# Part-array steps of the first group in larger sets: decode value sums, retention reads, state updates

## The chip, the core and the metric

The kernel runs on one core of a Trainium2 chip, in one launch. The metric is the device time in microseconds; three runs were made. A profile of one more execution shows every instruction with its start and length.

The core has five engines that work at the same time, each through its own instructions in order: TensorE (PE; its weight loads are shown as PEld), VectorE (DVE), ScalarE (ACT), GpSimd (POOL) and SyncE (SP, which only issues transfers here). Matmul results land in PSUM, which this kernel uses as eight banks of 128 x 512 fp32 values.

## The reference

One step of a layer with two groups of eight heads, 128 wide each, in fp32. A prompt of 1024 frames and eight running streams of 16 new frames ("sample") pass through it. Group A is stick-breaking attention, group B is retention with a state per head:

```python
def stick_breaking_block(q, k, v, q_start):
    z = einsum('bqhd,bkhd->bhqk', q, k) * HEAD_DIM ** -0.5
    strict = (k_pos[None, :] < q_pos[:, None])
    log_beta = log_sigmoid(z)
    log_keep = where(strict, log_sigmoid(-z), 0.0)
    later = cumsum(log_keep, axis=3, reverse=True) - log_keep
    a = where(strict, exp(log_beta + later), 0.0)
    return einsum('bhqk,bkhd->bqhd', a, v)

def retention_chunk(q, k, v, s, log_gamma):
    scores = einsum('bihd,bjhd->bhij', q, k) * intra
    o = einsum('bhij,bjhe->bihe', scores, v)
    o = o + einsum('bihd,bhde->bihe', q, s) * decay_read
    s_new = s * exp(lg * n) + einsum('bjhd,hj,bjhe->bhde', k, decay_write, v)
    return o, s_new

def reference(...):
    # prompt and sample alike:
    h = rms_norm(x, norm_pre)
    q_sb, k_sb, v_sb, gate_sb, q_r, k_r, v_r, gate_r = split(h @ w_in)   # 2048 x 8192; rope on q_r, k_r
    o_sb = stick_breaking(...)     # sample: over 1024 cached keys and values and its own 16
    o_r, s = retention(...)        # sample: from state_ret
    y = concat(head_rms_norm(o_sb) * silu(gate_sb), head_rms_norm(o_r) * silu(gate_r))
    x = x + rms_norm(y @ w_out, norm_post)
    # also returned: new keys, values and states
```

## The kernel before

Frames are taken in tiles of 128: eight of the prompt (0 to 7) and one that holds all eight sample streams (16 frames each). The first group is tiles 0 to 3 and the sample tile, the second is tiles 4 to 7. For each group the kernel goes through the eight heads. A head has its projections ("products", `products` and `project_rows`, lines 229 and 288): each is a long chain of matmuls over 16 input tiles, in three terms of a high and low split, into banks called `acc` or `accn`. A weight tile is loaded by SP (`wr`), split by ScalarE (`wh`) and VectorE (`wl`), four tiles ahead. After both groups comes the output projection.

Everything else of a head is cut into small steps and put between the products. A step sequence is a Python generator in a `Job`; it yields the number of ticks until its next step. `tick()` is called behind each term of products (every two products in the first group, every three in `project_rows`), and runs at most one due job. The constants `D_...` are these counts; those with two entries are for the two groups. A scheduler then sets the final order of each engine's instructions, which the order listings show.

The steps that the change touches are all in the first group, since only that one has the sample tile:

- `decode`: stick-breaking attention of the sample tile over the cache. Keys come in pieces (`kc`, by POOL), VectorE turns them (`kcT`), and twice per head a set of eight matmuls makes 512 columns of scores `zc`, for 32 rows of queries each, so four of them fill the array's columns. ScalarE evacuates them as `kp` and `be`. The weights are turned through DRAM; then the values: `pd` takes one matmul with the sample's own values (line 720) and eight key tiles of cached values `vc` (line 728), four matmuls of 32 rows each. These were written two key tiles at a time, `2 * D_VC` ticks apart. VectorE then puts together `do`.
- `sample_retention`: loads four tiles of states `st`, computes scores times values (line 812) and reads of the states (line 815, again 32 rows of the output each) into the accumulator bank `pa`, puts `ro` together on ScalarE and VectorE, and updates the states from keys of 32 frames (line 832): two sets of two tiles, in the two banks of the score pool `z`, each added to `st` by VectorE (line 835) and stored.
- `stick_breaking`: rows of prompt attention, lagged by two: scores `z` (line 588), weights turned through DRAM, and the sums with values into `pa` (line 618). `D_TR` is the pause before the last row's sums.

An fp32 matmul of these steps is two instructions in the profile. In the profile's shapes, 128*32 is a matmul on 128 rows and 32 columns of the array, 32*128 one on 32 rows and 128 columns.

## Time and profile before

| | |
|---|---|
| median of 3 runs | 2400.34 us (2395.4 to 2400.91) |
| the profiled execution | 2397.79 us, its span 2396.1 us |
| TensorE busy | 2332.6 us, 97% of the span |
| VectorE, ScalarE, GpSimd busy | 1254.6, 919.6, 646.2 us |
| mean granted TensorE clock | 0.993 of full speed |
| transfers | 418.68 MB, mean 175 GB/s |

The first group's heads run from about 165 to 1230 us. Start times in the timeline tell more than busy times here, because matmuls overlap one another in flight: the time that a step costs TensorE is read from the start of the product before it to the start of the product behind it.

### The profile page before, as it was taken

How to read it: one execution, taken by the hardware profiler on the slowest of the kernel's cores; microseconds unless marked ns; L12 is line 12 of the kernel's file. 1: busy time of each engine (PE TensorE's matmuls, PEld its weight loads, DVE VectorE, ACT ScalarE, POOL GpSimd, SP SyncE). 2: the span in 40 equal slices, each digit the busy share in tenths (PEclk: the TensorE clock that was granted, in tenths of full speed). 3: DMA queues.
4: the chain of work that ended last, by engine and by line, in shares of the span. 5: the costliest groups of instructions: out<-in, count | busy, mean ns of one | idle time of the engine just before them, and what ended most of it. 6: DMA issues, size and time to landing. Idle time of an engine off the chain costs nothing.

```text
span 2396.1 us, 40529 instructions
## 1 busy us (share of the span) xinstructions
PE 2332.6 (97%) x14832; PEld 2094.6 (87%) x14832; DVE 1254.6 (52%) x2442; ACT 919.6 (38%) x1937; POOL 646.2 (27%) x1033
## 2 busy tenths in 40 slices
PE   7999999999999999998899999999999999999998
PEld 7998899999999999987778888889898888888887
DVE  7245455445554555455545554555554566564544
ACT  6323333324333333324333343343343444444443
POOL 3144353444344353443302111120220220010000
PEclk9999999999999999999999999999999999999999
DMA  7658879797889879798875555556654667765553
GB/s 244 166 130 210 167 166 197 174 199 164 188 178 191 181 174 187 182 192 199 188 189 150 150 141 150 146 142 153 153 152 127 166 163 195 231 214 181 189 191 131
DMA packets 677050, 418.68 MB, mean 175 GB/s; under 512 B 224753, under 2 KB 620017, under 8 KB 674545
## 3 DMA queue, kind: packets, MB, share of 16 engines
q1 hardware_dynamic: 524272, 285.99, 47.6%
q0 software_dynamic: 32256, 71.36, 13.7%
q10 hardware_dynamic: 120320, 58.74, 9.0%
q8 instruction: 116, 1.90, 0.3%
q14 instruction: 86, 0.70, 0.1%
HBM read 336.24 MB, written 79.69 MB: 174 GB/s over the span
## 4 chain that ended last, share of the span: by engine, by line
PE 83%; DMA 7%; DVE 4%; issue 2%; ACT 2%; SPq 1%; POOL 0%; DVEq 0%; ACTq 0%; POOLq 0%
PE acc L229 44%; PE accn L288 17%; DMA mr<-s_y 4%; PE a L1031 3%; PE a L1032 3%; PE a L1030 3%; PE pa L618 3%; PE z L588 2%; DMA wr<-w_in 2%; PE zc L661 1%; PE pd L728 1%; DMA mr<-s_h 1%; DVE wl L132 1%; DVE ml L132 1%; ACT mh L131 1%
## 5 line engine op out<-in xcount | busy, mean ns | idle before, releaser
L229 PE MATMUL acc<-mh,wh 128*128 128x256 f32 (+2 forms) x2304 | 665.4, 342 | 7.8 <-ACT wh L131 5.0
L132 DVE TENSOR_TENSOR wl<-wr,wh 128x512 fp32r<-128x512 f32 (+1 forms) x576 | 391.8, 685 | 523.8 <-ACT wh L131 513.8
L229 PE MATMUL acc<-ml,wh 128*128 128x384 f32 (+2 forms) x2304 | 663.8, 341 | 0.0
L229 PE MATMUL acc<-mh,wl 128*128 128x256 f32 (+2 forms) x2304 | 660.2, 339 | 0.6 <-DVE wl L132 0.5
L131 ACT ACTIVATE wh<-wr 128x512 fp32r<-128x512 f32 (+1 forms) x576 | 357.4, 625 | 730.9 <-PE acc L229 247.7
L229 PEld LDWEIGHTS acc<-mh,wh 128*128 128x128 f32 x2304 | 420.7, 189 | 45.0 <-ACT wh L131 7.1
L229 PEld LDWEIGHTS acc<-mh,wl 128*128 128x128 f32 x2304 | 424.7, 189 | 31.6 <-issue 2.1
L229 PEld LDWEIGHTS acc<-ml,wh 128*128 128x128 f32 x2304 | 422.9, 189 | 33.2 <-issue 5.3
L645 POOL DMA_DIRECT2D kc<-cache_sb_k x512 | 331.6, 653 | 370.0 <-DVE kcT L683 205.9
L288 PE MATMUL accn<-whn,mh 128*128 128x256 f32 x1152 | 329.2, 287 | 0.6 <-ACT whn L131 0.5
L288 PE MATMUL accn<-wln,mh 128*128 128x256 f32 x1152 | 325.9, 283 | 1.5 <-DVE wln L132 1.5
L288 PE MATMUL accn<-whn,ml 128*128 128x256 f32 x1152 | 325.9, 283 | 0.0
L288 PEld LDWEIGHTS accn<-whn,mh 128*128 128x128 f32 x1152 | 220.5, 192 | 10.5 <-issue 7.5
L288 PEld LDWEIGHTS accn<-wln,mh 128*128 128x128 f32 x1152 | 220.9, 192 | 2.5 <-DVE wln L132 1.7
L288 PEld LDWEIGHTS accn<-whn,ml 128*128 128x128 f32 x1152 | 220.9, 192 | 0.0
L1031 PE MATMUL a<-wl,mh 128*128 128x512 f32 (+1 forms) x576 | 219.5, 381 | 0.2 <-DVE wl L132 0.2
L1032 PE MATMUL a<-wh,ml 128*128 128x512 f32 (+1 forms) x576 | 219.0, 381 | 0.0
L1030 PE MATMUL a<-wh,mh 128*128 128x512 f32 (+1 forms) x576 | 218.9, 381 | 0.0
L132 DVE TENSOR_TENSOR wln<-wrn,whn 128x512 fp32r<-128x512 f32 x128 | 87.5, 687 | 119.7 <-ACT whn L131 119.5
L131 ACT ACTIVATE whn<-wrn 128x512 fp32r<-128x512 f32 x128 | 80.1, 633 | 151.6 <-PE accn L288 65.4
L481 POOL DMA_DIRECT2D be<-s_be x128 | 94.0, 741 | 134.2 <-DMA s_be<-be 114.6
L1031 PEld LDWEIGHTS a<-wl,mh 128*128 128x128 f32 x576 | 108.4, 188 | 21.2 <-DVE wl L132 0.9
(189 smaller groups left out, 2611.6 us busy)
## 6 DMA issues: line engine op xcount, KB each, us to landing
wr<-w_in SPq DMA_DIRECT2D x384, 256.0 KB, 4.2
wr<-w_out SPq DMA_DIRECT2D x184, 256.0 KB, 3.6
wrn<-w_in SPq DMA_DIRECT2D x128, 256.0 KB, 3.2
kc<-cache_sb_k POOLq DMA_DIRECT2D x512, 64.0 KB, 4.6
vc<-cache_sb_v SPq DMA_DIRECT2D x64, 512.0 KB, 8.5
xt<-x_prompt SPq DMA_DIRECT2D x8, 1024.0 KB, 6.2
xr<-x_prompt SPq DMA_DIRECT2D x8, 1024.0 KB, 6.5
out<-out ACTq DMA_DIRECT2D x24, 256.0 KB, 3.6
```

Source lines behind the costliest of these rows:

```text
L131: nc.scalar.activation(hi, src, AF.Copy)
L132: nc.vector.tensor_tensor(lo, src, hi.bitcast(F32), ALU.subtract)
L229: last = nc.tensor.matmul(a[:, :m], lhs[:, j, :], rhs[w][:, j, o : o + m], start=(w == 0 and j == 0 and n == 0), stop=(w == KT // WQ - 1 a ...
L288: anchor[0] = nc.tensor.matmul(a, lhs[q][:, jj, ts], rhs[:, j, :], start=(w == 0 and j == 0 and n == 0 and t % 2 == 0), stop=(w == KT // 2 ...
L481: q.dma_start(raw[32 * i : 32 * i + 32, :].rearrange("p (k a) -> p k a", a=32), s[:, :, 32 * i : 32 * i + 32].rearrange("k (j b) a -> b (k ...
L588: nc.tensor.matmul(z[:, :c], q2[a][:, i * P : (i + 1) * P], k2[b][:, s : s + c], start=(m == 0), stop=(m == 2),)
L618: nc.tensor.matmul(po[:, :P], at[:, j, :], vn[:, j, :], start=(j == 0), stop=(j == t))
L645: nc.gpsimd.dma_start(kc[32 * i : 32 * i + 32, :].rearrange("p (k d) -> p k d", d=32), cache_k[0, 2 * c + j, s * 512 : (s + 1) * 512, h, 3 ...
L661: mm = nc.tensor.matmul(z[r, :], qp[:, j, r], ready[2 * j + c // 2][:, c % 2, :], start=(j == 0), stop=(j == 1),)
L1030: nc.tensor.matmul(a[:, :width], hi[q][:, j, ts], wh, start=(k == 0), stop=False)
L1031: nc.tensor.matmul(a[:, :width], hi[q][:, j, ts], wl, start=False, stop=False)
L1032: nc.tensor.matmul(a[:, :width], lo[q][:, j, ts], wh, start=False, stop=(k == KT - 1))
```

## The change

The value sums of a head go in two sets of four key tiles, 46 ticks apart, where there were four sets of two. The retention reads no longer stand at a place of their own: they are put in a list, and issued right behind the first set of decode scores that comes (`with_scores`), with the scores-times-values matmul behind them; head 0 keeps them where they were. If no set comes within 80 ticks they are issued anyway. The state updates go in one set with four tiles, two in the banks of the score pool, one in the accumulator bank `pa` and one in the decode bank `pd`; the order of the first two alternates by head, and the first matmuls are tied to stand in that order. The four stores follow after a pause. The pause before the last attention row in the first group is 12 ticks instead of 3, the one before the value sums 7 instead of 3, and the decode sums on VectorE wait six ticks more.

```diff
-D_TR = (3, 7)
+D_TR = (12, 7)
-D_VC = 9
+D_VC = (6, 46)
+V_SET = 4
+D_SUM = 6
+D_TD = 7
+D_OFF = 3
+N_READ = 40
...
+        waiting = []
+        def with_scores():
+            while waiting:
+                waiting.pop(0)()
...
                     ready = []
+                    with tc.issue_after(mm.ins):
+                        with_scores()
                     sigmoids(kp, be, s * 512, z)
...
-            yield D_TR[phase[0]]
+            yield D_TD
...
-            for k0 in range(0, 8, 2):
-                yield 2 * D_VC
-                for k in (k0, k0 + 1):
+            for k0 in range(0, 8, V_SET):
+                yield D_VC[k0 > 0]
+                for k in range(k0, k0 + V_SET):
                     vc = values.pop(0)
...
+            yield D_SUM
             od = out.o[:, 0, :]
...
-            po = acc_tile()
-            nc.tensor.matmul(po[:, 2 * P : 3 * P], sc, rv[:, i, :], start=True, stop=True)
-            for c in range(4):
...
-            yield D_RET[phase[0]]
+            def read_states():
+                po = acc_tile()
+                for c in range(4):
+                    r = slice(32 * c, 32 * c + 32)
+                    nc.tensor.matmul(
+                        po[r, : 2 * P], rq[:, i * P + 32 * c : i * P + 32 * c + 32], sts[c], start=True, stop=True
+                    )
+                nc.tensor.matmul(po[:, 2 * P : 3 * P], sc, rv[:, i, :], start=True, stop=True)
+                read.append(po)
+            if h:
+                waiting.append(read_states)
+                for _ in range(N_READ):
+                    if read:
+                        break
+                    yield 2
+            if not read:
+                waiting.clear()
+                read_states()
+            po = read[0]
+            yield D_OFF
...
-            for c0 in (0, 2):
-                pS = [score_tile(f"pSs{c}", (P, 2, P)) for c in range(2)]
...
+            yield D_OFF
+            pS = [score_tile(f"pSs{c}", (P, 2, P)) for c in range(2)]
+            pS += [
+                pool.tile([P, 512], F32, name=f"p{n}", tag=f"p{n}")[:, : 2 * P].rearrange("p (j e) -> p j e", j=2)
+                for pool, n in ((psa, "a"), (psd, "d"))
+            ]
+            lead = None
+            for j in range(2):
+                for c in (0, 1, 2, 3) if h % 2 else (1, 0, 2, 3):
+                    r = slice(32 * c, 32 * c + 32)
+                    with tc.issue_after(lead.ins) if lead else nullcontext():
+                        mm = nc.tensor.matmul(pS[c][:, j, :], rkn[r, i + j, :], rv[r, i, :], start=True, stop=True)
+                    if j == 0 and c < 2:
+                        lead = mm
+            for c in range(4):
+                nc.vector.scalar_tensor_tensor(
+                    sts[c], sts[c], math.exp(LOG_GAMMA[h] * DS), pS[c], ALU.mult, ALU.add
+                )
+            yield D_RET[phase[0]]
+            for c in range(4):
+                nc.scalar.dma_start(s_sample[0, 2 * c : 2 * c + 2, h].rearrange("b d e -> d b e"), sts[c])
```

The new order is read at three places, all in the head with index 4 of the first group (one of the middle heads); products are left out.

TensorE, from the value sums of that head to the first retention steps of the next, before the change (`pd` are the value sums, `rs` retention scores, `pa` the accumulator bank):

```order
L720 MATMUL pd<-vn,kp 128x128
L728 MATMUL pd<-vc,kp 32x256 x8
...
L728 MATMUL pd<-vc,kp 32x256 x8
...
L728 MATMUL pd<-vc,kp 32x256 x8
...
L754 MATMUL rs<-rq,rk 128x128
...
L754 MATMUL rs<-rq,rk 128x128
...
L728 MATMUL pd<-vc,kp 32x256 x8
...
L772 MATMUL pa<-rv,sc 128x128
```

The same stretch of TensorE after the change:

```order
L733 MATMUL pd<-vn,kp 128x128
L741 MATMUL pd<-vc,kp 32x256 x16
...
L741 MATMUL pd<-vc,kp 32x256 x16
...
L768 MATMUL rs<-rq,rk 128x128
...
L768 MATMUL rs<-rq,rk 128x128
```

Four sets of eight matmuls, with 34 to 36 products between them, have become two of sixteen with 76 products between them, and none stands behind the retention scores any more.

TensorE at the reads and updates, before (`pSs` are the update tiles, `zc` the decode scores):

```order
L812 MATMUL pa<-rv,sc 128x128
L815 MATMUL pa<-st,rq 32x256 x4
...
L832 MATMUL pSs_8266<-rv,rkn 128x128
L832 MATMUL pSs_8267<-rv,rkn 128x128
...
L832 MATMUL pSs_8315<-rv,rkn 128x128
...
L661 MATMUL zc<-kcT,qp 32x512 x8
```

and after (`z` are the scores of a prompt row):

```order
L672 MATMUL zc<-kcT,qp 32x512 x8
L831 MATMUL pa<-st,rq 32x256 x4
L834 MATMUL pa<-rv,sc 128x128
...
L866 MATMUL pSs_8375<-rv,rkn 128x128
L866 MATMUL pSs_8374<-rv,rkn 128x128
L866 MATMUL pa<-rv,rkn 128x128
L866 MATMUL pd<-rv,rkn 128x128
...
L593 MATMUL z<-kh,qh 128x256
```

The reads follow the scores with nothing between; 21 products stand between them and the one update set, and three products between that set and the next `z`, which takes the bank of the first update tile. Here the updates stood before the decode scores, now they stand behind them.

VectorE at the same place, before (`ro` is the retention output, `ov` and `or` its norm, `st` the states):

```order
L822 SCALAR_TENSOR_TENSOR ro<-pa,dec,ro 128x128 x2
L683 STREAM_TRANSPOSE kcT<-kc 128x512
L132 TENSOR_TENSOR wln<-wrn,whn 128x512
L139 TENSOR_SCALAR ov<-ssq_7506 128x5
L835 SCALAR_TENSOR_TENSOR st<-st,pSs_8266 128x256
L835 SCALAR_TENSOR_TENSOR st<-st,pSs_8267 128x256
L141 RECIPROCAL or<-or 128x5
```

and after:

```order
L851 SCALAR_TENSOR_TENSOR ro<-pa,dec,ro 128x128 x2
L696 STREAM_TRANSPOSE kcT<-kc 128x512
L144 TENSOR_SCALAR ov<-ssq_7498 128x5
L146 RECIPROCAL or<-or 128x5
L870 SCALAR_TENSOR_TENSOR st<-st,pSs_8375 128x256
L870 SCALAR_TENSOR_TENSOR st<-st,pSs_8374 128x256
L902 STREAM_TRANSPOSE kn<-kT 128x640
L870 SCALAR_TENSOR_TENSOR st<-st,pa 128x256
L870 SCALAR_TENSOR_TENSOR st<-st,pd 128x256
```

The reciprocal, which waits for ScalarE's square root, now stands ahead of the first update, and a transposition of keys stands between the second and the third.

More of the change, by code (lines that the diff above doesn't have):

```diff
@@ L730, in decode @@
                         )
-                for k in (k0, k0 + 1):
+                for k in range(k0, k0 + V_SET):
                     if k + V_BUFS < 8:
                         values.append(load_v(k + V_BUFS))
+            yield D_SUM
             od = out.o[:, 0, :]
@@ L825, in sample_retention @@
             out.done(i)
-            for c0 in (0, 2):
-                pS = [score_tile(f"pSs{c}", (P, 2, P)) for c in range(2)]
-                for j in range(2):
-                    for c in range(2):
-                        r = slice(32 * (c0 + c), 32 * (c0 + c) + 32)
-                        nc.tensor.matmul(pS[c][:, j, :], rkn[r, i + j, :], rv[r, i, :], start=True, stop=True)
-                for c in range(2):
-                    st, b = sts[c0 + c], 2 * (c0 + c)
-                    nc.vector.scalar_tensor_tensor(
-                        st, st, math.exp(LOG_GAMMA[h] * DS), pS[c], ALU.mult, ALU.add
-                    )
-                    nc.scalar.dma_start(s_sample[0, b : b + 2, h].rearrange("b d e -> d b e"), st)
-                yield D_RET[phase[0]]
+            yield D_OFF
[19 more added lines that the diff above has]
+                nc.scalar.dma_start(s_sample[0, 2 * c : 2 * c + 2, h].rearrange("b d e -> d b e"), sts[c])
         def ret_branch(gi, g, h, rq, rk, rv, rest):
```

5 lines of the change are left out of this document (1 added, 4 removed).

## The prediction

> **What bounds the kernel now.** I read the page first, then the list of waits and the table by stretch for the middle heads of the first group, then the timeline of TensorE around each kind of step that the change touches, and last the timelines of ScalarE and VectorE behind the retention reads. The page gives each engine's busy time (share of the span) and the chain that ended last:
>
> ```profile
> PE 2332.6 (97%) x14832; PEld 2094.6 (87%) x14832; DVE 1254.6 (52%) x2442; ACT 919.6 (38%) x1937; POOL 646.2 (27%) x1033
> PE 83%; DMA 7%; DVE 4%; issue 2%; ACT 2%; SPq 1%; POOL 0%; DVEq 0%; ACTq 0%; POOLq 0%
> ```
>
> TensorE is the bound, but "busy" counts a matmul in flight, so a pause in which the array drains does not show there. The table by stretch (heads 1 to 6 of the first group in the first row, two pieces of head 7 below; the numbers are length, busy time of each engine, the granted TensorE clock, DMA share, GB/s) and the list of TensorE's waits (total, times, longest; two rows of heads 1 to 6, then one of heads 0 and 1) are these:
>
> ```profile
> 330.00:1075.00 745.00, 742.40 (x5576) 696.79 (x5578) 384.44 (x803) 253.39 (x552) 323.93 (x538) 1.00 0.85 184
> 1110.00:1120.00 10.00, 7.62 (x41) 5.04 (x39) 5.43 (x11) 4.56 (x10) 7.94 (x14) 0.83 1.02 248
> 1120.00:1135.00 15.00, 12.33 (x84) 9.46 (x81) 9.81 (x24) 4.94 (x11) 5.34 (x9) 0.89 0.77 165
> ```
> ```profile
> PE pa L772 <- DVE sc L756: 0.8, 2, 0.4
> PE pa L618 <- DVE kb L578: 0.7, 3, 0.2
> PE pa L772 <- DVE sc L756: 3.3, 1, 3.3
> ```
>
> In heads 1 to 6 TensorE is busy for 742.4 of 745 us at full clock, so whatever shortens its own queue there shortens the run. What can be shortened is read from start times.
>
> **Value sums.** TensorE's timeline (start, length of the merged record, instructions), around a set that ran with 32 instructions and one that ran with 16, both of head 0:
>
> ```profile
> 249.89 0.46 PE L229 MATMUL acc<-ml,wh 128*128 128x256 f32 x2
> 250.18 0.38 PE L720 MATMUL pd<-vn,kp 128*128 128x128 f32 x2
> 250.50 1.94 PE L728 MATMUL pd<-vc,kp 128*32 128x256 f32 x32
> 252.36 0.56 PE L229 MATMUL acc<-mh,wl 128*128 128x256 f32 x2
> 252.76 0.46 PE L229 MATMUL acc<-mh,wh 128*128 128x256 f32 x2
> ...
> 255.41 0.46 PE L229 MATMUL acc<-mh,wh 128*128 128x256 f32 x2
> 255.79 1.07 PE L728 MATMUL pd<-vc,kp 128*32 128x256 f32 x16
> 256.79 0.56 PE L229 MATMUL acc<-ml,wh 128*128 128x256 f32 x2
> 257.19 0.45 PE L229 MATMUL acc<-mh,wl 128*128 128x256 f32 x2
> ```
>
> A pair of products keeps a pace of 0.29 (249.89 to 250.18). From 255.41 to 257.19 are 1.78 us with two pairs in them, so the set of 16 costs 1.20. In the records of 16 and of 32 the difference is 1.94 - 1.07 = 0.87, which is the price of 16 instructions without entering and leaving. So each visit to the narrow shape has a fixed part of 1.20 - 0.87 = 0.33 us, before and behind it, in which the array empties and fills.
>
> The next row counts the instructions of these sums in the whole run; the one under it is the update of the sample states:
>
> ```profile
> L728 PE MATMUL pd<-vc,kp 128*32 128x256 f32 x512 | 33.9, 385 | 0.0
> L832 PE MATMUL pSs<-rv,rkn 32*128 32x128 f32 x128 | 11.9, 297 | 2.7 <-DVE st L835 2.7
> ```
>
> 512 instructions are 28 sets of 16 and the two of 32 that the scheduler had joined (heads 0 and 7): 30 visits. Afterwards the loop makes two sets of 32 per head, 16, and in the new order head 7's second set is cut in three: 18. Twelve visits fewer. I count eleven, 11 x 0.33 = **3.6 us**: head 0's gain runs into the 3.3 us wait quoted last in the list, which is for VectorE behind a transfer. Cover: the seventh and eighth value tile are loaded once the first set has freed their buffers, and 76 products then pass until the second set needs them, 38 pairs of 0.29 = 11.0 us. A load takes, from issue:
>
> ```profile
> vc<-cache_sb_v SPq DMA_DIRECT2D x64, 512.0 KB, 8.5
> ```
>
> So some 2 us of cover remain; without it each microsecond late is paid in full, in eight heads. SP's queue holds these loads in the same place relative to the weight loads or two loads later, which costs nothing while four weight tiles are ahead.
>
> In six heads the step ahead of the first set was late:
>
> ```profile
> 785.39 0.46 PE L229 MATMUL acc<-ml,wh 128*128 128x256 f32 x2
> 785.92 0.46 PE L720 MATMUL pd<-vn,kp 128*128 128x128 f32 x2
> 786.31 1.07 PE L728 MATMUL pd<-vc,kp 128*32 128x256 f32 x16
> ```
>
> It starts 0.53 after the pair where 0.29 would do, and takes 0.39 to the set where head 0 takes 0.32: 0.31 us lost. D_TD lets four more ticks (eight products, 1.2 us) pass before it, so the wait goes: 6 x 0.3 = **1.8 us** (0.5 to 1.8; what is late next is the turned row of weights, by the same transfer). The last attention row is moved nine ticks later (D_TR) for the same reason: I take the 0.7 us of the wait list, **0.7 us** (0 to 1.5). D_SUM moves three VectorE steps by six ticks; nothing waits for them in that head: nothing.
>
> **Reads and updates.** The timeline around one head's reads, and around one of its two update sets:
>
> ```profile
> 568.98 0.39 PE L812 MATMUL pa<-rv,sc 128*128 128x128 f32 x2
> 569.30 0.64 PE L815 MATMUL pa<-st,rq 128*32 128x256 f32 x8
> 569.87 0.56 PE L229 MATMUL acc<-mh,wh 128*128 128x256 f32 x2
> 570.26 0.46 PE L229 MATMUL acc<-ml,wh 128*128 128x256 f32 x2
> ```
> ```profile
> 572.32 0.46 PE L229 MATMUL acc<-mh,wl 128*128 128x256 f32 x2
> 572.71 0.71 PE L832 MATMUL pSs<-rv,rkn 32*128 32x128 f32 x8
> 573.35 0.56 PE L229 MATMUL acc<-mh,wh 128*128 128x256 f32 x2
> 573.75 0.46 PE L229 MATMUL acc<-ml,wh 128*128 128x256 f32 x2
> ```
>
> Reads: 1.28 from the first row to the last, less a pair (0.29), less the eight instructions themselves (half of 0.87, 0.43), less two full-width ones (0.22), leaves 0.33 again. The scores that they are now put behind have the same narrow shape (both read 128*32), so the reads need no visit of their own: seven heads x 0.33 = **2.3 us**. Head 0 keeps its own visit.
>
> Updates: 1.43 with two pairs is 0.84 for a set of eight, twice per head. One set of sixteen uses four row groups and four banks. If all four work side by side, it costs what eight cost on two, and 0.84 is saved; if they queue, the starts, which spread over 0.71 - 0.27 = 0.44 for eight, spread twice as far, and 0.40 is saved. The nearest row with four parts at work is the value sum, whose 16 further instructions of 256 columns cost 0.87, 0.054 each, a quarter of the 0.22 that twice a full-width 128-column one takes: all four parts at once. So I take 0.84: 7 x 0.84 = **5.9 us** (2.8 to 5.9), head 0 again left out. The Trainium skill (TensorEngine Tiling (Array Packing), Theoretical Speedup) promises up to four times the throughput for contractions of at most 32; by it the 5.9 stands, by the pairs that the trace shows it would be 2.8.
>
> **The wait that is added.** The two update tiles of the score pool now hold both of its banks, and three products later a new score z wants one. It must wait for VectorE's first update, and VectorE has a reciprocal ahead of it, which waits for ScalarE. The rows of ScalarE and VectorE behind the reads above, then ScalarE's after a set of scores in the same head:
>
> ```profile
> 570.08 0.28 ACT L820 ACTIVATE ro<-pa 128x128 f32<-128x128 f32 x1 [1.44 <-PE pa L815]
> 571.58 1.28 ACT L140 ACT_TABLE_LOAD   x1
> 573.12 0.19 DVE L141 RECIPROCAL or<-or 128x5 f32<-128x5 f32 x1 [0.63 <-ACT or L140]
> ```
> ```profile
> 583.18 0.59 ACT L500 ACTIVATE kp<-zc 128x512 f32<-128x512 f32 x1
> 584.13 0.41 ACT L500 ACTIVATE kb<-z 128x256 f32<-128x256 f32 x1
> ```
> ```profile
> L835 DVE SCALAR_TENSOR_TENSOR st<-st,pSs 128x256 f32<-128x256 f32 x32 | 12.1, 414 | 8.6 <-PE pSs L832 8.1
> ```
>
> From the copy to the end of the reciprocal are 3.2 us. The copy now stands behind both score evacuations, 0.95 later (583.18 to 584.13). So the first update ends about 0.1 + 0.95 + 3.2 + 0.4 = 4.7 us behind the scores. TensorE wants its bank after the reads (0.4), the full-width pair (0.2), 21 products (2.5 at the 256-column pace, 3.1 at 0.147), the set (0.84) and three products (0.4): 4.3 to 4.9. I take 0.2 us in six heads, **-1.2 us** (0 to -3.5). Queued behind z are only products; ScalarE evacuates z ahead of the eight key stores and again behind them, and the next z comes 90 products (10.7 us) later, so those stores and the four state stores, moved behind the updates, stay covered. The accumulator bank is needed by the set's third matmul, 3.3 us after the scores; its readers are done before the table load begins, 0.1 + 0.95 + 1.5 (570.08 to 571.58) = 2.6: no wait.
>
> **Head 7** held two waits of the steps that change, and the clock fell behind each:
>
> ```profile
> 1113.28 2.85 PE L815 MATMUL pa<-st,rq 128*32 128x256 f32 x8 [2.38 <-DMA st<-state_ret]
> 1126.11 0.71 PE L832 MATMUL pSs<-rv,rkn 32*128 32x128 f32 x6 [2.67 <-DVE st L835]
> ```
>
> The waits are 5.0 us; granted 0.83 of 10 us and 0.89 of 15 us, the clock cost 1.7 + 1.65. The reads now come 82 products behind the last score piece, when the states have landed, and the second update set is gone; but ScalarE and VectorE are late there anyway, and one z is now evacuated between reads and update. I take half of 8.4, **4.2 us** (-3 to 8.4).
>
> **Sum:** 3.6 + 1.8 + 0.7 + 2.3 + 5.9 - 1.2 + 4.2 = **17.3 us**. The profiled execution took 2397.79 us (span 2396.1), 2.6 below the median of the runs, 2400.34; the sum is 2380.5 on its own time and **2383.0** on the median. The ends of the terms add to 23.5 and 2.7: 2377 and 2398.
>
> **Rivals.** (a) *Small gain*: the row groups queue (-3.1) and head 7 keeps its waits (-4.2): 10.0 us, 2390. For it: two row groups at once is all that the trace shows. Chance 0.2. (b) *No change*: transfers set the pace, since the DMA share in heads 1 to 6 is 0.85, and TensorE's gain turns into waits for weights; about 2397. Against it: the wait list of that stretch names under 2 us in 745. With it I count that a few terms fail together. Chance 0.14. (c) *Slower*: the bank wait is not 0.2 but some 3 us, because VectorE also stands at a key transpose ahead of the reciprocal, whose loads can be late. Above some 2.4 us the clock falls too, 1.7 us as in head 7: 6 x (3 + 1.7) = 28 us against 13 gained outside head 7 without this term: about +14, 2414. It decides once the wait passes the 2.1 us that a middle head gains. The Trainium skill warns of this side (TensorEngine Tiling (Array Packing), PSUM Bottleneck): after a fourfold faster array the evacuation can become the bottleneck; the row has 4 x 0.41 = 1.65 us of VectorE behind a set of 0.84. Chance 0.1. The forecast itself has 0.56.
>
> **Numbers.** About 0.3%, 7 us, is what a measurement of this kernel can tell from no change (its own runs lie from 2395.4 to 2400.91). Below 2393.1 lie the forecast and most of (a): faster 0.75. Within: (b) and the rest of (a), 0.15. Slower: (c), 0.10. The range, 2374 to 2397, takes the ends of the terms and the lower of the runs, and leaves out (c) and part of (b).
>
> **What would show it.** Right: 18 value-sum visits; no visit for reads outside head 0; an update record of 16 about 0.7 us long; no wait for L720's step; a wait of z for VectorE's update under 0.5 us; heads 1 to 6 shorter by 2 us each. Wrong: an update record of 1.1 us or more, z waiting over 2 us, TensorE waiting for value tiles, or a granted clock below 1.00 in heads 1 to 6.

## The result, and the profile after

The changed kernel takes 2393.5 us (median of 21 runs, 2388.74 to 2400.81) beside 2397.12 for the kernel before in the same runs (21 runs, 2392.09 to 2404.21): ratio 0.9986, 95% interval 0.9978 to 0.9993. It is 3.6 us faster, where 17.3 were forecast. The profiled execution took 2393.5 us, its span is 2391.8.

The page after: busy times, and the chain that ended last.

```profile
PE 2320.5 (97%) x14832; PEld 2092.4 (87%) x14832; DVE 1255.6 (52%) x2442; ACT 920.0 (38%) x1937; POOL 644.1 (27%) x1033
PE 71%; DMA 6%; DVE 4%; issue 2%; ACT 2%; SPq 1%; POOL 0%; DVEq 0%; ACTq 0%; POOLq 0%
```

TensorE is busy 12.1 us less than before. The table by stretch, with the columns and stretches of the prediction, shows that it isn't full any more: in heads 1 to 6 there are 8.4 us without a matmul in flight (before: 2.6), and head 7's first row is at 0.75 clock.

```profile
330.00:1075.00 745.00, 736.62 (x5605) 699.57 (x5604) 387.25 (x812) 255.09 (x555) 322.34 (x535) 1.00 0.87 185
1110.00:1120.00 10.00, 5.46 (x31) 3.48 (x33) 5.30 (x10) 4.07 (x10) 7.47 (x12) 0.75 0.98 271
```

The groups of instructions (busy, mean ns of one, idle before them) and TensorE's timeline in one head show the steps as forecast: the value sums' 512 instructions, the reads right behind the scores, and an update set of sixteen on banks of three pools (`pSs`, `pa`, `pd`), all started within 0.5 us.

```profile
L741 PE MATMUL pd<-vc,kp 128*32 128x256 f32 x512 | 33.1, 387 | 4.2 <-DMA vc<-cache_sb_v 4.2
L866 PE MATMUL pSs<-rv,rkn 32*128 32x128 f32 x64 | 6.2, 298 | 0.0
```
```profile
580.40 0.28 PE L293 MATMUL accn<-whn,ml 128*128 128x256 f32 x1
580.61 1.92 PE L672 MATMUL zc<-kcT,qp 128*32 128x512 f32 x16
582.35 0.61 PE L831 MATMUL pa<-st,rq 128*32 128x256 f32 x8
582.90 0.49 PE L834 MATMUL pa<-rv,sc 128*128 128x128 f32 x2
...
583.34 0.28 PE L293 MATMUL accn<-wln,mh 128*128 128x256 f32 x1
...
585.62 0.28 PE L293 MATMUL accn<-whn,ml 128*128 128x256 f32 x1
585.83 0.38 PE L866 MATMUL pSs<-rv,rkn 32*128 32x128 f32 x2
585.84 0.37 PE L866 MATMUL pa<-rv,rkn 32*128 32x128 f32 x1
585.85 0.37 PE L866 MATMUL pd<-rv,rkn 32*128 32x128 f32 x1
...
586.28 0.27 PE L866 MATMUL pd<-rv,rkn 32*128 32x128 f32 x1
...
586.71 0.28 PE L293 MATMUL accn<-wln,mh 128*128 128x256 f32 x1
...
587.21 0.39 PE L593 MATMUL z<-kh,qh 128*128 128x256 f32 x1
```

So where did the gain go? TensorE's waits in heads 1 to 6 (total, times, longest) have a row that was 0.8 us before:

```profile
PE pa L786 <- DVE sc L770: 6.5, 4, 3.9
PE pd L733 <- DVE or L146: 1.2, 1, 1.2
```

`sc` is the decayed copy of the retention scores. The longest of these waits, on TensorE's timeline and on VectorE's:

```profile
544.84 0.79 PE L786 MATMUL pa<-rv,sc 128*128 128x128 f32 x2 [3.85 <-DVE sc L770]
```
```profile
539.82 0.85 DVE L887 STREAM_TRANSPOSE rkn<-ro 128x640 f32<-128x640 f32 x1 [0.47 <-DMA ro<-s_rk]
543.14 0.71 DVE L556 STREAM_TRANSPOSE kT<-so 128x512 f32<-128x512 f32 x1
544.50 0.49 DVE L770 TENSOR_TENSOR sc<-rs,dT 128x128 f32<-128x128 f32 x2 [0.65 <-DMA dT<-c_dt]
```

VectorE takes its work in order: the transposition of the turned retention keys (waits for their transfer), other steps, then `sc`, which waits for the decay table `dT`. The keys are first written out to DRAM (their turn-out) and then read back turned. The read-back and the table are SyncE's. Its queue there, after and then before (start and length of the issues):

```profile
514.63 4.33 SPq L220 DMA_DIRECT2D wr<-w_in  x1
519.04 3.93 SPq L702 DMA_DIRECT2D vc<-cache_sb_v  x2
525.74 1.91 SPq L220 DMA_DIRECT2D wr<-w_in  x2
527.70 6.20 SPq L486 DMA_DIRECT2D ro<-s_rk  x4
534.01 4.60 SPq L486 DMA_DIRECT2D so<-s_o  x4
538.66 1.31 SPq L763 DMA_DIRECT2D dT<-c_dt  x1
```
```profile
520.62 5.99 SPq L481 DMA_DIRECT2D ro<-s_rk  x4
526.71 2.06 SPq L481 DMA_DIRECT2D so<-s_o  x4
528.81 0.56 SPq L749 DMA_DIRECT2D dT<-c_dt  x1
```

Two weight loads more than before now stand ahead of the keys (one in every second head), and the table is issued 9.9 us later than before, or 12.1 us counted from the head's newest-key scores `zn`. The loads are not the whole of it: counted the same way, the turn-out landed at 42.6 us instead of 35.2, and the keys were issued 2.0 us behind it; their own issues and those behind them took longer too.

Head 7 is the other place. The two waits of the steps that change are gone, and others stand in their stead; the two longest rows of TensorE's waits from 1060 to 1260 us (`rg` is the gate, made by ScalarE and VectorE from the bank of the gate's products):

```profile
PE acc L234 <- ACT wh L136: 6.9, 2, 5.2
PE accn L293 <- DVE rg L320: 4.5, 1, 4.5
```

By stretch of the profiled runs, in us, cut where each head's newest-key scores `zn` start (head 0's `zn` to head 1's is "head 1", and so on):

| kernel | to head 0 | head 1 | heads 2 to 6 | head 7 | rest | span |
|---|---|---|---|---|---|---|
| before | 220.5 | 131.6 | 670.9 | 154.6 | 1218.4 | 2396.1 |
| after | 218.9 | 133.3 | 668.1 | 150.7 | 1220.8 | 2391.8 |
| update set alone (e1) | 218.0 | 136.1 | 662.7 | 144.5 | 1219.7 | 2381.0 |
| reads alone (e2) | 220.9 | 134.9 | 686.9 | 148.8 | 1219.3 | 2410.8 |
| keys early (e4) | 219.0 | 133.0 | 658.8 | 151.9 | 1222.7 | 2385.4 |
| head 7's reads back (e7) | 218.9 | 134.2 | 669.0 | 145.0 | 1219.4 | 2386.4 |
| update, sums, keys early (e12) | 216.5 | 134.5 | 657.4 | 143.8 | 1222.7 | 2374.9 |

Each row is one execution, and single executions lie apart: e4's here was 4.0 us faster than the median of its eight runs. In the changed kernels `zn` also stands up to 16 products earlier or later in the order than before (2.3 us at 0.147 each), so neighbouring stretches trade some us.

### The profile page after: what moved, and what is told of

The parts are those of the page before. It is cut to its first block, busy times and chain, and to the rows that moved or that the text cites. A ratio compares the mean times of both kernels' runs of the same rounds, so it can differ in the third digit from the quotient of the medians.

```text
span 2391.8 us, 40520 instructions
## 1 busy us (share of the span) xinstructions
PE 2320.5 (97%) x14832; PEld 2092.4 (87%) x14832; DVE 1255.6 (52%) x2442; ACT 920.0 (38%) x1937; POOL 644.1 (27%) x1033
## 4 chain that ended last, share of the span: by engine, by line
PE 71%; DMA 6%; DVE 4%; issue 2%; ACT 2%; SPq 1%; POOL 0%; DVEq 0%; ACTq 0%; POOLq 0%
PE acc L234 36%; PE accn L293 12%; PE a L1067 5%; PE a L1066 5%; PE a L1068 5%; PE pa L623 2%; PE z L593 2%; DMA wr<-w_in 2%; PE zc L672 1%; PE pd L741 1%; DMA mr<-s_y 1%; DMA mr<-s_h 1%; DMA dT<-c_dt 1%; DVE wl L137 1%; PE pa L786 1%
## 5 line engine op out<-in xcount | busy, mean ns | idle before, releaser
L234 PE MATMUL acc<-ml,wh 128*128 128x256 f32 (+2 forms) x2304 | 661.5, 339 | 0.0
L293 PEld LDWEIGHTS accn<-whn,mh 128*128 128x128 f32 x1152 | 220.9, 192 | 8.5 <-DVE rg L320 4.8
L1066 PE MATMUL a<-wh,mh 128*128 128x512 f32 (+1 forms) x576 | 218.9, 381 | 0.1
L1068 PE MATMUL a<-wh,ml 128*128 128x512 f32 (+1 forms) x576 | 218.9, 380 | 0.0
```

The source lines that it names most:

```text
L234: last = nc.tensor.matmul(a[:, :m], lhs[:, j, :], rhs[w][:, j, o : o + m], start=(w == 0 and j == 0 and n == 0), stop=(w == KT // WQ - 1 a ...
L293: anchor[0] = nc.tensor.matmul(a, lhs[q][:, jj, ts], rhs[:, j, :], start=(w == 0 and j == 0 and n == 0 and t % 2 == 0), stop=(w == KT // 2 ...
L1066: nc.tensor.matmul(a[:, :width], hi[q][:, j, ts], wh, start=(k == 0), stop=False)
L1068: nc.tensor.matmul(a[:, :width], lo[q][:, j, ts], wh, start=False, stop=(k == KT - 1))
```

## The experiments

All ratios are to the kernel before on the same chip, with their 95% interval.

**The three parts alone.** e1 has only the update set, e2 only the reads, e3 only the value sums.

Each edit's core, in that order (e3 has the change's constants, without the later last row):

```diff
-for c0 in (0, 2):
-    pS = [score_tile(f"pSs{c}", (P, 2, P)) for c in range(2)]
+pS = [score_tile(f"pSs{c}", (P, 2, P)) for c in range(2)]
+pS += [
...
+    for pool, n in ((psa, "a"), (psd, "d"))
+]
```
```diff
-yield D_RET[phase[0]]
+if h:
+    waiting.append(read_states)
```
```diff
-for k0 in range(0, 8, 2):
-    yield 2 * D_VC
+for k0 in range(0, 8, V_SET):
+    yield D_VC[k0 > 0]
```

> The kernel before with one part of the change alone: the four states of a head are updated in one set of sixteen matmuls on four banks, instead of two sets of eight. Theory A (the savings on TensorE are real, and part of them was given back because the turned retention keys and the decay table stand two weight loads later in SyncE's queue): this part's saving is 7 x 0.84 us = 5.9 us, and it puts the keys one weight load later, not two, so it keeps 3 to 6 us of it: ratio to before 0.9975 to 0.9987. Theory B (transfers set the pace of the first group, so what TensorE saves comes back as waits whatever is saved): within 1.5 us of before, ratio 0.9994 to 1.0006. Theory C (the value sums in sets of four are the part that costs): 5 to 6 us faster, ratio 0.9975 to 0.998.

Measured: 2382.75 us, 0.9946 (0.9934 to 0.9958): 13.3 us faster, more than any theory had. TensorE's list of waits is empty in heads 1 to 6, and the row of the table by stretch has it busy for 744.4 of 745 us:

```profile
330.00:1075.00 745.00, 744.40 (x5630) 700.26 (x5630) 389.07 (x821) 256.42 (x561) 324.81 (x538) 1.00 0.86 186
```

Theory B falls: what TensorE saves does shorten the run. Of the 15.1 us between the two rows of the table, 3.7 come from heads 1 to 6 together (six sets of 0.84 are 5.0), 8.8 from head 7 and what follows, and 2.5 from ahead of head 0.

> The kernel before with one part of the change alone: the reads of the retention states stand behind a head's second set of decode scores. Theory A: the saving is 7 x 0.33 us = 2.3 us, less what one weight load ahead of the turned keys costs: 0 to 2.3 us faster, ratio 0.999 to 1.000. Theory B: within 1.5 us of before. Theory C: 2.3 us faster, ratio 0.999.

Measured: 2412.75 us, 1.0071 (1.0058 to 1.0085). All three expected no loss: all missed. In heads 2, 4 and 6 TensorE waits for turned cache keys, as its list of waits in heads 1 to 6 shows; below it VectorE's and ScalarE's timeline ahead of one of these waits:

```profile
PE zc L672 <- DVE kcT L696: 9.2, 3, 3.3
```
```profile
489.72 0.63 ACT L136 ACTIVATE wh<-wr 128x512 fp32r<-128x512 f32 x1 [5.77 <-DMA wr<-w_in]
490.39 0.69 DVE L137 TENSOR_TENSOR wl<-wr,wh 128x512 fp32r<-128x512 f32 x1 [5.18 <-ACT wh L136]
492.82 0.70 DVE L696 STREAM_TRANSPOSE kcT<-kc 128x512 f32<-128x512 f32 x1
```

The keys' transposition stands behind a split weight on VectorE, that waits for ScalarE, and ScalarE for the weight's transfer.

> The kernel before with one part of the change alone: the decode value sums in sets of four key tiles with their new distances; the last attention row stays where it was. On TensorE it saves 11 x 0.33 + 1.8 us = 5.4 us. Theory A: it puts the turned keys two weight loads later, which costs some 5 us, so it ends within 2 us of before: ratio 0.9992 to 1.0008. Theory B: within 1.5 us of before, so not told from A by this run alone. Theory C: 3 to 6 us slower, ratio 1.001 to 1.0025.

Measured: 2407.47 us, 1.0043 (1.0028 to 1.0057): 11.5 us slower, which no theory had; the waits for `sc` are there (6.9 us), as A said, and 3.5 us for turned cache keys. The parts don't add: 13.3 less 16.7 less 11.5 would be 15 us slower, the whole is 3.6 faster. So what one part costs depends on the others.

**The turned keys early (e4).**

After, with 24 and 40 for the two pauses of 32 around the read-back.

```diff
-yield D_TO[phase[0]]
+yield 24 if gi == 0 else D_TO[phase[0]]
...
 turn_in(s, raw, nc.sync)
-yield D_TI[phase[0]]
+yield 40 if gi == 0 else D_TI[phase[0]]
```

> The changed kernel, with the turned retention keys of the first group read back 24 steps after they are sent out instead of 32, and the step behind it 40 instead of 32, so that the transposition keeps its place: in SyncE's queue the keys stand ahead of two weight loads again, as they did before the change. Theory A: the waits of TensorE for the decayed scores (6.5 us in heads 1 to 6) go, and the stretch between heads 3 and 4 shortens by the 3.9 us of its wait and the 1.7 us of half clock behind it: 4 to 8 us faster than the changed kernel, ratio to before 0.995 to 0.997. Theory B and theory C: as the changed kernel, ratio 0.998 to 0.9995.

Measured: 2391.17 us, 0.9979 (0.9969 to 0.9989). The waits for `sc` in heads 1 to 6 went entirely, and heads 2 to 6 are 9.3 us shorter than after (658.8 against 668.1), five heads at 131.8, or 2.4 each below before, where the forecast had 2. But head 7 and the rest lost 3.1 us in that profile. By the ratios e4 is only 1.7 us faster than after, and the two intervals overlap: the waits as A had them, the gain not shown.

**Two parts together (e5, e6).** e5 is e1 with e2's edit; e6 is e1 with e3's edit and this:

```diff
-D_TR = (3, 7)
+D_TR = (12, 7)
```

> The kernel before with two parts of the change: the one update set and the reads behind the scores; the value sums and the last attention row stay as before. Update set alone was 13.3 us faster than before (ratio 0.9946), reads alone 16.8 us slower. Theory A (parts cost or save by where they push the queues and by which waits they cover: the reads cost at head 7, where they no longer stand between the gate products and the value products that wait for the gate's bank, 4.5 us and 3.3 us of half clock in the trace after): 2.3 us saved and some 7 us lost against the update set alone, ratio 0.996 to 0.9975. Theory D (the reads cost some 17 us wherever they are put behind the scores): ratio 1.000 to 1.003. Theory E (parts just add, by their savings on TensorE): ratio 0.9935.

> The kernel before with two parts of the change: the one update set, and the value sums in sets of four with the last attention row later; the reads stay before the scores. Theory A: the turned keys stand two weight loads later and TensorE waits some 5 to 7 us for the decayed scores in heads 1 to 6, against 5.4 us saved, and head 7 keeps its cover: ratio 0.9935 to 0.996. Theory D (only the reads cost): 5 us faster than the update set alone, ratio 0.992 to 0.9935. If the sums cost by themselves what they did alone, 11.5 us: ratio 0.998 to 1.000.

Measured: e5 2386.86 us, 0.9964 (0.9953 to 0.9976), the number of A; e6 2388.35, 0.9968 (0.9955 to 0.9980), between A and its rival. Both are slower than the update set alone. In heads 1 to 6 TensorE's list of waits has no row for `sc` in e5; in e6 it has this one:

```profile
PE pa L778 <- DVE sc L762: 10.1, 6, 2.5
```

So the waits for `sc` come with the sums, not with the reads. A's place for e5's loss was wrong: against the update set alone its heads 1 to 6 took 8.2 us more (807.0 against 798.8), and head 7 with what follows 3.2 less, although the wait for `rg` is there (3.9 us). What the reads cost in heads 1 to 6 is taken up with e17.

**Head 7's cover (e7, e8).** e7 is after with one edit, e8 has e4's as well.

```diff
-            if h:
+            if 0 < h < H - 1:
                 waiting.append(read_states)
```

> The changed kernel, with the reads of head 7 alone put back to their own time, ahead of its decode scores, as head 0 has them in the change. Theory A: TensorE's wait of 4.5 us for the gate's bank in head 7 and the half clock in the scores behind it (8 x 0.41 = 3.3 us) go, so 4 to 8 us faster than the changed kernel: ratio to before 0.995 to 0.997. Rival (another wait stands right behind, as TensorE only arrives earlier at the same transfers): as the changed kernel, ratio 0.998 to 0.9995.

> The changed kernel with both: the turned keys of the first group ahead of two weight loads again, and the reads of head 7 at their own time. Theory A: heads 1 to 6 at 131.7 us each as with the early keys, against 132.7 us with the update set alone, and head 7 as with the update set alone (144 us): 5 to 8 us faster than the update set alone would be too much by what the rest after head 7 lost (3 us), so 2 to 6 us faster than it: 2377 to 2381 us, ratio 0.992 to 0.994. Rival: no better than the early keys alone, ratio 0.997 to 0.9985.

Measured: e7 2386.04 us, 0.9960 (0.9949 to 0.9972), so 6.2 us less than after by the ratios, with intervals that lie apart, as A. The wait for `rg` is gone; head 7 went from 150.7 to 145.0. In after, the products `accn` followed on the gate's products at once and waited for the bank that the gate step reads, and the scores behind that wait ran at half clock (a record of 3.64 us, where 1.92 is quoted above). The reads and the updates had stood ahead of `accn`, and had hidden it. The gate step was late by itself: the gate's products had ended at 1111.8 us, and on ScalarE the step stood behind splits of input tiles that waited for their transfer.

```profile
1113.39 1.22 ACT L136 ACTIVATE mh<-mr 128x512 fp32r<-128x512 f32 x2 [3.15 <-DMA mr<-s_h]
...
1115.03 0.75 ACT L319 ACTIVATE rg<-acc 128x256 f32<-128x256 f32 x2
```

Measured: e8 2385.07 us, 0.9958 (0.9946 to 0.9970), not told from e7, and outside both forecasts: with head 7's keys early too, TensorE waits there 4.9 us for split keys, and head 7 takes 154.0. Cover gained at one place was lost at another.

**Both, with head 7's keys left alone (e9).** As e8, with another condition for both pauses:

```diff
-yield 24 if gi == 0 else D_TO[phase[0]]
+yield 24 if gi == 0 and 0 < h < H - 1 else D_TO[phase[0]]
```

> The changed kernel, with the turned keys early in heads 1 to 6 only, and the reads of head 7 at their own time. With the keys early in head 7 too, two weight tiles of head 7 landed late and TensorE waited 4.9 us for the split keys there. Theory A (queue places and lost covers are the whole of it): heads 1 to 6 at 131.7 us as with the early keys, the stretch of head 7 at 145 us as with its reads alone put back: some 7 us faster than with the keys early in all heads, 2376 to 2380 us, ratio 0.9918 to 0.994. Rival (head 7 waits for something in any order, as transfers set its pace): 2383 to 2387 us, ratio 0.995 to 0.9965.

Measured: 2385.37 us, 0.9947 (0.9931 to 0.9962), between the two forecasts. By the ratios that is 9.3 us less than after, with intervals that lie apart, but only 3.1 less than e7, with intervals that overlap. Heads 2 to 6 kept their gain (659.9, 132.0 each), head 7 took 147.4 and the rest 1224.2: 1371.6 for both, where the update set alone has 1364.2. What A missed lies behind head 6.

**Is it the place in the queue? (e10, e11, e12).** e10 is e1 with e4's edit, but 36 and 28 for 24 and 40; e11 is after with the table loaded ahead of the pause before the keys, in both groups; e12 is e6 with the early keys of e9. The edits of e10 and e11:

```diff
-yield D_TO[phase[0]]
+yield 36 if gi == 0 else D_TO[phase[0]]
```
```diff
+tied(nc.sync.dma_start(dT, c_dt[:, h]))
 yield D_TO[phase[0]]
...
 turn_in(s, raw, nc.sync)
...
-tied(nc.sync.dma_start(dT, c_dt[:, h]))
```

> The kernel before with the one update set, and only the turned keys moved: they stand one more weight load later in SyncE's queue in heads 1 to 6 (read back 36 steps after they are sent out, not 32, the step behind it 28, not 32), the place that the whole change gives them. The update set alone had no wait of TensorE of 0.2 us or more in heads 1 to 6. Theory A: waits for the decayed scores appear, 5 to 10 us in all, and the kernel is 5 to 10 us slower than the update set alone: 2387 to 2393 us, ratio to before 0.9965 to 0.9985. Rival (the value sums themselves, not the keys' place, make the waits): as the update set alone, 2382 to 2384 us, ratio 0.994 to 0.9955.

> The changed kernel, with the decay table loaded before the turned keys are read back (some nine DMAs earlier in SyncE's queue); the keys themselves stay where the change put them. Theory A as the late keys: VectorE's transposition of the keys still stands ahead of the decayed scores in its order, so the waits stay: 6 us of waits in heads 1 to 6, ratio to before 0.998 to 0.9995. If the decay table is what comes last: 4 to 6 us faster than the changed kernel, ratio 0.996 to 0.9975.

> The update set, the value sums in sets of four and the later last row, the reads before the scores, with the turned keys early in heads 1 to 6. With the keys late this had 10.1 us of waits for the decayed scores. Theory A: they go, and the sums' own saving of 5.4 us is left: 2377 to 2380 us, ratio to before 0.992 to 0.994. Rival (the sums cost by something else too): 2383 to 2388 us, ratio 0.9948 to 0.997.

Measured, on one chip: e10 2380.45 us, 0.9926 (0.9913 to 0.9939); e11 2411.8, 1.0057 (1.0045 to 1.0069); e12 2378.51, 0.9918 (0.9904 to 0.9932), the fastest of all and, by the ratios, some 16 us below after, though not told from e10. e12 came out as A; e10 was faster and e11 slower than either forecast. The row for `sc` in TensorE's waits of heads 1 to 6, of e10, e11 and e12:

```profile
PE pa L777 <- DVE sc L761: 0.8, 1, 0.8
```
```profile
PE pa L784 <- DVE sc L768: 16.8, 5, 4.1
```
```profile
PE pa L778 <- DVE sc L762: 1.1, 2, 0.7
```

e10 refutes A as it stood: it has as many weight loads ahead of the keys as after has in heads 2 to 7, one more than the update set alone, and they cost nothing. Read from the start of a head's `zn` (heads 3 to 6), the turn-out of the keys is issued at 27.2 us in e10 and at 29.9 to 30.0 in e6; the table has landed at 52.0 to 53.6 and at 56.7 to 57.0; TensorE wants `sc` at 54.9 and, without the wait, at 56.4. The sums push the supply some 4 us back, the demand 1.5. The place alone still fits (e10); with the later turn-out it doesn't. A later turn-out alone was not run. e12 issues the keys at 36.3 to 37.9, as soon as the turn-out has landed (36.2 to 37.9), and fits again. e11 shows that an early table doesn't help by itself: it landed by 39 us, and `sc` still followed the keys' transposition, whose transfer had slipped to 54 to 55 us.

**What was still open (e13 to e16).**

e13 is e6 with a longer pause behind the first retention scores, e14 is e3 and e15 is e1 with the early keys of e9, e16 is e12 with sets of two in head 0. The edits of e13 and e16:

```diff
 sc = scores(0, 0)
-yield D_RET[phase[0]]
+yield 15 if gi == 0 and 0 < h < H - 1 else D_RET[phase[0]]
```
```diff
+vset = V_SET if h else 2
...
-yield D_VC[k0 > 0]
+yield D_VC[k0 > 0] if h else 18
```

> The update set with the value sums in sets of four (keys late, 10.1 us of waits for the decayed scores in heads 1 to 6, ratio 0.9968), and in heads 1 to 6 the first retention step 15 instead of 9 steps long, so that products of the next projection stand on TensorE between the retention scores and the product that needs their decayed copy, where a visit of the value sums stood before. The keys keep their place in SyncE's queue. Theory A2 (the wait is there because that cover went and the keys go out later, not by the queue's order alone): the waits go, and the kernel comes near the one with early keys: ratio to before 0.992 to 0.9945. Rival (only earlier keys help, since what waits for the keys on VectorE holds other work too): waits move to other products, ratio 0.996 to 0.998.

> The value sums in sets of four alone, with the turned keys early in heads 1 to 6; states updated in two sets and read before the scores as before the change. Alone, with the keys late, the sums were 11.5 us slower than before (6.9 us of waits for the decayed scores, 3.5 us for turned cache keys). Theory A2: the waits for the decayed scores go and with them the half clock behind them, 7 to 12 us: ratio to before 0.998 to 1.0013. Rival (the sums cost by something else as well): ratio 1.002 to 1.0045.

> The update set alone, with the turned keys early in heads 1 to 6. The update set alone had no wait of TensorE of 0.2 us or more in heads 1 to 6. Theory A2: nothing to be had from early keys where the cover stands, so as the update set alone within 2 us: ratio to before 0.993 to 0.9955. Rival (early keys save time by themselves, as transfers come in a better order): 5 us or more faster than the update set alone, ratio below 0.9925.

> The fastest so far (update set, sums in sets of four, keys early in heads 1 to 6, ratio 0.9918), with the value sums of head 0 in four sets of two at their old distances. In head 0 TensorE waits 2.9 to 4.2 us for value tiles with the sets of four and not at all in the kernel before. If that is a loss of its own: 1 to 4 us faster, ratio 0.990 to 0.9915. If it only takes the place of another wait of head 0 (the 5 us for the turned weights of the last row): the same, ratio 0.9915 to 0.993, or slower by the two visits that come back, 0.7 us.

Measured, on one chip: e13 2401.36 us, 1.0016 (1.0005 to 1.0027), slower than both forecasts. It settles nothing on the cover: in its waits of heads 1 to 6 `sc` is still there, and cache keys now too.

```profile
PE zc L666 <- DVE kcT L688: 8.2, 3, 3.7
PE pa L778 <- DVE sc L762: 7.9, 5, 2.0
```

e14 2402.22, 1.0027 (1.0014 to 1.0040): the waits for `sc` fell from 6.9 to 0.2 us, but the 3.5 us for cache keys stayed, so the sums alone cost something else too, as the rival had it. e15 2389.33, 0.9967 (0.9955 to 0.9980), some 5 us slower than the update set alone, which neither forecast had: early keys gain nothing where nothing waits, and what they cost shows in no wait of heads 1 to 6 and stays open. e16 2382.46, 0.9933 (0.9920 to 0.9946), not faster than e12: the 2.9 us that head 0 waits for value tiles in e12 only takes the place of other waits (4.8 us for `sc` there in e16). In heads 1 to 6 of e16 `sc` is waited for again, 4.7 us in four waits, with the keys early: the early place does not always do.

**Why the reads cost (e17).** In e2's heads with the wait, SyncE issues the two first value tiles 16 to 19 us ahead of `zn`, before the weight loads, and a weight issued behind them takes up to 12.3 us to land. e17 is e2 with:

```diff
+if h:
+    yield 10
 values = [load_v(k) for k in range(2)]
```

> The reads behind the scores alone (as in the second run, ratio 1.0071), with the first two value tiles of heads 1 to 7 loaded ten steps later, behind two to four weight loads in SyncE's queue in heads 3 to 7; the newest decode scores, written behind these loads, come ten steps later too. If the value tiles ahead of the weights are the cause: TensorE's waits of 9.2 us for turned cache keys go, with the half clock behind them, and the kernel is 8 to 14 us faster than the reads alone: ratio to before 1.001 to 1.004. If the reads themselves or something else are the cause: the waits stay, ratio 1.006 to 1.010.

Measured: 2398.62 us, 1.0002 (0.9992 to 1.0012), a little better than the forecast. The weights of heads 2 to 6 land within 10.1 us, the reads' 17 us are gone, and so is the wait, as the same row shows:

```profile
PE zc L672 <- DVE kcT L696: 0.3, 1, 0.3
```

So most of it came with where the value tiles are loaded, not with the reads as such. That the order of value tiles and weights was the whole cause is not shown: the edit moves the newest scores and what follows them by ten steps as well, in before a weight took up to 11.3 us at this place without any such wait, and heads 1 to 6, cut at the same product of TensorE, take 802.5 us before, 819.8 in e2 and still 809.0 in e17.

## Why the prediction was right or wrong

- **Sign and range** held, the range only at its edge: 3.6 us is little more than the 2.7 us to which its low ends add, and the terms of TensorE's work did not come out low. That the time itself lies inside is in part luck: the range stood on a kernel before of 2400.34 us, and its 21 runs gave 2397.12. The size didn't hold: 3.6 us for 17.3, within the 0.3% that rival (b) was given, but for another reason. (b) said that transfers set the pace whatever is saved; e1, e10 and e12 show that savings can arrive. (In rival (c), the 13 us gained outside head 7 are 14.3 by the terms.)
- **Value sums**: 18 visits, as counted. Reckoned as in the prediction, a set of 32 costs 2.65 us less two pairs, 2.07, against twice 1.20 for two sets of 16: 0.33 a visit, as forecast. The rows are of one of the middle heads:

```profile
667.81 0.45 PE L234 MATMUL acc<-ml,wh 128*128 128x256 f32 x2
668.20 1.93 PE L741 MATMUL pd<-vc,kp 128*32 128x256 f32 x32
...
670.46 0.46 PE L234 MATMUL acc<-mh,wh 128*128 128x256 f32 x2
```

The wait before the step of L733 (L720 before) is down to one of 1.2 us. The cover of some 2 us held in heads 1 to 6, not in head 0: TensorE waits there 4.2 us for value tiles, one of the signs of being wrong.
- **Updates**: the set of sixteen costs 0.85 us from start to start, the eight cost 0.84: four row groups run side by side, and 5.9 us was right as a term of TensorE (rival (a)'s half fell). Alone the part gave 13.3, since head 7 lost waits as well; that 4.2-us term was too small for it and too large for the whole.
- **Reads**: scores and reads cost 2.48 us together (580.40 to 583.34, less two products of 0.12 and the full-width pair of 0.22). Apart the reads were 0.77, as in the prediction, and the scores 2.04 by these rows of before (2.28 less two products). So 0.33 a head, as forecast.

```profile
578.42 0.28 PE L288 MATMUL accn<-whn,ml 128*128 128x256 f32 x1
578.63 1.92 PE L661 MATMUL zc<-kcT,qp 128*32 128x512 f32 x16
...
580.70 0.28 PE L288 MATMUL accn<-wln,mh 128*128 128x256 f32 x1
```

- **The added wait** of z (-1.2) came, about as sized. In six heads z starts 0.26 us later than the pace (586.71 to 587.21 with one product of 0.12 between, where 0.24 would do), 1.6 us in all. Its weight load waits for VectorE's update:

```profile
587.20 0.19 PEld L593 LDWEIGHTS z<-kh,qh 128*128 128x128 f32 x1 [0.31 <-DVE st L870]
```

Rival (c) didn't come. The Trainium skill's warning of it (TensorEngine Tiling (Array Packing), PSUM Bottleneck) bound here by no more than these 0.26 us a head; the rest of the 1.65 us of evacuation stayed hidden.
- **The step that failed** is the sentence on SP's queue: loads "in the same place relative to the weight loads or two loads later, which costs nothing while four weight tiles are ahead". It asked only whether weights would be late. Behind those loads stand the turned keys and the decay table, with some 2 us to spare (in e1 the table has landed by 52.6 us, and `sc` is wanted at 54.5), and VectorE's order ties `sc` to both. With the value sums the table comes some 4 us later, by the loads and by the later turn-out, and `sc` is wanted only 1.5 us later: waits of 6.5 us, one of them with 1.6 us of half clock behind it, a granted clock below 1.00 in heads 1 to 6, which was another sign of being wrong. What the early keys are worth depends on the rest: some 12 us from e6 to e12 (0.9968 against 0.9918, the one pair whose intervals lie apart), 1.7 to 3.8 from after to e4, from e7 to e9 and from e3 to e14, and from e1 to e15 a loss of 5.
- **Head 7** (+4.2) failed too, and here the changed kernel itself shows it: the term counted the waits that go, and put at nothing the cover that the moved reads gave. They had covered a bank wait of 4.5 us, and without them half clock followed; with them back (e7) the kernel is 6.2 us faster. In the profiles head 7 was 3.9 us shorter than before, and 2.4 were given back behind it.
- **Both undone** (e9) give back 9.3 of the 13.7 us that were missing; the other 4.4 stay open.
- **Head 0** (nothing): 1.6 us gained up to its `zn`, 1.7 lost by the next.
- **Open**: why early keys cost 5 us beside the update set alone, why they gain so little in after, and what makes e9 slower than e12. Head 7 lay between 143.8 and 154.6 us with nearly the same work on TensorE.

## What to carry to other kernels

When steps move in a kernel whose queues run in order, cost what stands behind them in each queue, down to the last consumer's slack: a place in the queue that is harmless by itself can, together with another small delay, push a small table past its need. A step that is taken away may have been the cover of a wait; ask what the two neighbours that now meet share. And try each part alone: here one of three parts was worth more than the whole, and the whole with the keys loaded earlier and the reads left out was worth over five times as much.

## What was unexpected of the hardware

How long a wait was did not by itself decide whether the clock fell behind it. The rows of the table by stretch (length, busy times, clock, DMA share, GB/s) are those behind the wait of 3.85 us in after, behind one of 2.23 us in e3 and behind one of 3.34 us in e2:

```profile
545.00:548.40 3.40, 3.40 (x14) 3.40 (x15) 2.97 (x6) 1.57 (x4) 0.32 (x2) 0.52 1.20 228
```
```profile
679.70:682.70 3.00, 2.96 (x12) 2.96 (x13) 2.85 (x7) 1.24 (x4) 1.22 (x2) 0.52 1.19 240
```
```profile
1041.70:1044.70 3.00, 2.98 (x16) 2.14 (x17) 1.15 (x2) 1.43 (x4) 2.00 (x5) 1.00 0.30 83
```

Clock 0.52, 0.52 and 1.00: the prediction's "above some 2.4 us the clock falls" does not hold. From 330 to 1260 us of all these profiles every wait of TensorE above 3.4 us was followed by a lower clock, and of those between 1.9 and 3.4 us some were and some weren't. Behind the longest wait in after, the half clock lasted 3.4 us and cost 1.6. The Trainium skill (TensorE: Matmul & The Clock Gate, What's actually happening) gives about 3.4 us of activity until full clock; the trace agrees there.

Issuing can itself be slow: SyncE needed 4.33 us for one weight load and 6.20 for four small ones in the rows above, where the median issue of a weight load in heads 1 to 6 took 0.39. The DMA share from 515 to 548 us was 1.06; that the crowd of transfers is the reason is not shown. And a transfer waits on the issuing engine: in e12 the turn-outs landed at 36.2 to 37.9 us and the keys were issued at 36.3 to 37.9, right behind them, and the loads written behind the keys came later still. The Trainium skill says the same, in a section on GpSimd's transfers (DMA: Bandwidth & Descriptors, Anatomy of one DMA — SWDGE (gpsimd) path): any wait for a semaphore happens on the issuing sequencer.
